# Sums of weight blocks formed by accumulating transfers, and five products of each FFN cut in two

## The chip, the cores and the metric

The kernel runs on one core of a Trainium2 chip. The metric is the device time of one execution in microseconds. A comparison uses the median of several runs.

## The reference

A decoder trunk of two layers over 256 positions of width 1024, in float32. Each layer has an FFN, a token-mixing sub-layer (a state-space branch and a delta-rule branch side by side), and a second FFN. The change touches only the four FFNs:

```python
def swiglu(x, w_in, w_out):
    gate, up = jnp.split(x @ w_in, 2, axis=-1)
    return (jax.nn.silu(gate) * up) @ w_out

for l in range(DEPTH):
    h = h + 0.5 * swiglu(rms_norm(h, ffn1_norm[l]), ffn1_w_in[l], ffn1_w_out[l])
    u = rms_norm(h, mix_norm[l])
    ...
    h = h + merged @ w_out[l]
    h = h + 0.5 * swiglu(rms_norm(h, ffn2_norm[l]), ffn2_w_in[l], ffn2_w_out[l])
return rms_norm(h, final_norm)
```

The inner width is 2816, that is 22 rows of 128 channels in `w_out`.

## The kernel before

**Numbers in two parts.** TensorE multiplies values of the type fp32r, which hold fewer bits than float32. So each float32 value is split into a high part, which ScalarE (ACT) makes by a copy, and a low part, which VectorE (DVE) makes by a subtraction. A product is three matmuls: high by high, high by low, low by high (`mm3`, `mm3w`). Weights are split on the chip: a raw tile of 128 x 1024 (512 KB) is loaded into `wraw` (five buffers, NRAW), `prep` makes `whi` and `wlo` (five buffers each, NSPL), and a product takes the pair with `take`.

**The plan.** `stream` lists the raw tiles in the order of their loads, and `plan` lists the forms in the order in which the products use them. `take` returns form j; before that it records the loads that are to be ahead of it and the `prep` of the forms up to j + 4. Each engine has a queue of its own that runs in order. The scheduler fills a queue by priority, which is program order, but when the next instruction has no free buffer it passes to a later one that has.

**An FFN** is the list `FFN`: one unit `f` with tokens as stationary side, then 20 units `c` (`chan_chunk`, two for each of ten channel pairs, 48 matmuls of 256 columns each), four block stages `A`, and the tail `BdBBBddddd`. `A` stands behind the 8th, 12th, 16th and 18th unit. Of the 22 rows of `w_out`, 16 are handled as eight pairs `PAIRS` by a scheme with seven instead of eight products of 2 x 2 blocks: rows are split in two channel blocks, columns in two halves of 512, tokens in two halves of 128. The activation's sums (`block_sums`) are made by DVE and ACT when a channel pair is done. The weights' sums are made from raw tiles that hold one block of two pairs: with b11, b12, b22 and b21 for the blocks, the products use b11, b12 - b11, b22 - b12 and b22 - b12 + b11 in `A` (forms `q0` to `q3`), and b22, b21 and b21 - b22 + b12 - b11 in `B` (`q4` to `q6`). A running sum lives in the tile `wfirst`, one of four slots `y0` to `y3` that are also used by the mixer. The subtractions are `less` in `prep`, on DVE: one each beside `q0`, `q1`, `q2` and `q4`, so 16 in an FFN. Those of `q1`, `q2` and `q4` stand between the ACT copy and the DVE split of that form.

Matmuls of a unit: for each half `a` of the channels, eight steps `kt` of three matmuls (L301 to L303) into one accumulator `fc`. Those of a block are L296 to L298 into `p` (stage `A`) or `o` (the tail). `join` adds the block accumulators into `h`; `close_blocks` runs the tail and ends with a group of five direct chunks. All other rows, `d`, are direct (`out_chunks`). All loads are issued by SyncE's queue (SP, L147). GpSimd (POOL) has little to do: the power in each norm (L190), a few others of the mixer.

Of the kernel before, what the change touches and what calls it, by code (L numbers as in the profile page):

```python
# [7 lines left out]
F32 = mybir.dt.float32  # L8
# [44 lines left out]
def trunk_kernel(ctx, tc, x, wst, wsm, norms, lpar, rpar, cst, out):  # L53
# [15 lines left out]
    def tt(o, a, b, op):  # L69
        return V.tensor_tensor(out=o, in0=a, in1=b, op=op)  # L70
# [29 lines left out]
    def plan_plain(j, n):  # L100
        for i in range(j, j + n):
            stream.append(i)
            plan.append(("d", [len(stream) - 1], len(stream)))
        return j + n

    def plan_ffn(j):


        o, j2, held = j + 4 * FC, j + 4 * FC + 22, []
        for kind in FFN:  # L110
            if kind in "fc":
                j = plan_plain(j, 4 if kind == "f" else 2)
            elif kind == "d":
                o = plan_plain(o, 1)
            else:
                if kind == "A":
                    where = [len(stream) + i for i in range(3)]
                    stream.extend(range(o, o + 3))
                    held.append((where, o + 2))
                    o += 4  # L120
                    for i, need in enumerate((2, 3, 3, 3)):
                        plan.append((f"q{i}", where, where[0] + need))
                else:
                    where, b22 = held.pop(0)
                    where += [len(stream) + 1, len(stream)]
                    stream.extend([b22, b22 + 1])
                    for i in range(4, 7):
                        plan.append((f"q{i}", where, len(stream)))
        return j2
# [6 lines left out]
    first = {js[0] for kind, js, _ in plan if kind == "q0"}  # L136
# [3 lines left out]

    def load(j):
        if j in first:
            r = slots.tile([P, 1024], F32, tag=f"y{state['first']}", name="wfirst")
# [3 lines left out]
        state["last"] = nc.sync.dma_start(r[:], wst[stream[j] // 2, :, (stream[j] % 2) * 1024 :][:, 0:1024])  # L147
        raws[j] = r

    def prep(i):  # L150
        kind, js, _ = plan[i]
        hi = wpool.tile([P, 1024], F32R, tag="whi", name="whi", bufs=NSPL)
        lo = wpool.tile([P, 1024], F32R, tag="wlo", name="wlo", bufs=NSPL)

        def less(o, a, b):
            tt(raws[js[o]][:], raws[js[a]][:], raws[js[b]][:], ALU.subtract)


        r = raws[js[{"q2": 1, "q4": 4, "q5": 3}.get(kind, 0)]]
        with ExitStack() as behind:  # L160
            for ins in state["behind"].pop(i, ()):
                behind.enter_context(tc.issue_after(ins))
            act(hi[:], r[:])
            if kind == "q1":
                less(1, 2, 1)
            elif kind == "q2":
                less(0, 2, 0)
            elif kind == "q4":
                less(0, 3, 0)
            tt(lo[:], r[:], f(hi[:]), ALU.subtract)  # L170
            if kind == "q0":
                less(0, 1, 0)
        for o in {"d": (0,), "q2": (1,), "q3": (2,), "q4": (4,), "q5": (3,), "q6": (0,)}.get(kind, ()):
            raws.pop(js[o])
        halves[i] = (hi, lo)

    def ahead(key, n, fn):
        while state[key] < n:
            fn(state[key])
            state[key] += 1  # L180

    def take():
        j = state["taken"]
        state["taken"] = j + 1
        ahead("loaded", min(plan[min(j + NSPL, n_forms) - 1][2] + NRAW - 1, n_raw), load)
        ahead("prepped", min(j + 1 if state["hold"] else j + NSPL, n_forms), prep)
        return halves.pop(j)
# [112 lines left out]
    def mm3w(ps, wh, wl, mh, ml, start, stop):  # L300
        PE.matmul(ps, wh, mh, start=start, stop=False)  # L301
        PE.matmul(ps, wh, ml, start=False, stop=False)  # L302
        PE.matmul(ps, wl, mh, start=False, stop=stop)  # L303
# [18 lines left out]
    def chan_chunk(ps):  # L322

        ws = [take(), take()]
        for a in range(2):
            for q in range(2):
                wh, wl = ws[q]
                for k in range(4):
# [9 lines left out]
                        kt == KT - 1,  # L338
                    )
# [48 lines left out]
    def join(pb):  # L388
# [6 lines left out]
        stt(u4[:], pb[5][:], 0.5, u2[:], ALU.mult, ALU.add)  # L395
        tt(hv[0][1], hv[0][1], u4[:], ALU.add)
        yield
        stt(u2[:], pb[7][:], 0.5, u2[:], ALU.mult, ALU.add)
        stt(u5[:], pb[5][:], 0.5, u2[:], ALU.mult, ALU.add)
        tt(hv[1][0], hv[1][0], u2[:], ALU.add)  # L400
        tt(hv[1][1], hv[1][1], u5[:], ALU.add)
# [27 lines left out]
    def ffn(nxt):  # L429
# [19 lines left out]
        def block_sums(p, g2):  # L449
# [34 lines left out]
        todo, pb, n = FFN[1:], {}, 0  # L484
        for c in range(FC - 1):
            g2 = tmp2("g2")
            for a in range(2):
                ps = accb("fc")
                chan_chunk(ps)
# [13 lines left out]
            if todo[0] == "A":  # L503
                if not pb:
                    pb.update({i: trb(f"p{i}") for i in (1, 6, 5, 7)})
# [7 lines left out]
                todo = todo[1:]  # L513
# [845 lines left out]
```

## Time and profile before

| | before |
|---|---|
| median of 3 runs | 1576.33 us (1573.42 to 1577.17) |
| the profiled execution's own time | 1574.73 us |
| span of that execution | 1573.0 us |
| TensorE busy | 1544.0 us, 98% |
| VectorE busy | 1254.2 us, 80% |
| ScalarE busy | 950.7 us, 60% |
| GpSimd busy | 53.8 us, 3% |
| read from HBM | 289.33 MB, 185 GB/s over the span |

How to read the lines: a group line gives the source line, the engine, the operation, the tile it writes and those it reads, the shape, the count, then the busy time in us, the mean of one in ns, and the engine's idle time ahead of it with what ended that. In a line of a stretch, each engine has its busy us and its count of instructions that touch the stretch; then come the clock that TensorE was granted (1.00 is full), the mean busy share of the 16 DMA engines, and GB/s. In a line in order of time, the first number is the start in us from the start of the span and the second is the duration; a bracket at the end gives the idle time before it and what released it. PE is TensorE and PEld its weight loads.

### The profile page before, as it was taken

The numbers are of one execution on the slowest core, as the hardware profiler recorded it, in microseconds if no ns is written. First come the engines' busy times: TensorE is split into PE (matmuls) and PEld (weight loads), VectorE is DVE, ScalarE is ACT, GpSimd is POOL, SyncE is SP. The second block draws the span as 40 slices with busy tenths as digits, with TensorE's granted clock in tenths as the row PEclk, the third lists the DMA queues.
The fourth block names the chain that finished last, engine by engine and source line by source line (L and its number), as shares of the span: only waits on it lengthen the run. The fifth ranks groups of instructions, "written<-read, shape, count | busy, mean of one in ns | idle before, by whom it ended". The sixth has DMA issues, their size and how long they took to land.

```text
span 1573.0 us, 28904 instructions
## 1 busy us (share of the span) xinstructions
PE 1544.0 (98%) x11432; PEld 1393.4 (89%) x11432; DVE 1254.2 (80%) x1888; ACT 950.7 (60%) x1534; POOL 53.8 (3%) x60
## 2 busy tenths in 40 slices
PE   8999999999999999999999999999999999999997
PEld 7999779999888888999789997899998888899995
DVE  6878868967899766878777888699589987677887
ACT  5656568766666645555555566776756665455554
POOL 0000010000000000000000001010000000000000
PEclk9999999999999999999999999999999999999999
DMA  8565565553565566565765456555345556555554
GB/s 297 199 201 186 185 213 188 168 164 114 180 212 164 183 205 192 169 207 181 243 206 191 166 186 223 192 188 188 115 137 200 175 185 215 176 191 187 161 186 133
DMA packets 94221, 293.12 MB, mean 186 GB/s; under 512 B 22325, under 2 KB 23301, under 8 KB 93062
## 3 DMA queue, kind: packets, MB, share of 16 engines
q1 hardware_dynamic: 94086, 291.29, 56.5%
q8 instruction: 89, 1.46, 0.4%
q14 instruction: 46, 0.38, 0.1%
HBM read 289.33 MB, written 1.92 MB: 185 GB/s over the span
## 4 chain that ended last, share of the span: by engine, by line
PE 68%; DVE 14%; DMA 7%; issue 5%; ACT 4%; POOL 1%; SPq 0%; POOLq 0%; ACTq 0%; DVEq 0%
PE fc L301 9%; PE fc L302 9%; PE fc L303 9%; DVE wlo L70 7%; DMA wraw<-in_wst_dram 4%; PE b L298 3%; PE t L297 3%; PE t L296 2%; PE t L298 2%; PE b L297 2%; PE b L296 2%; DVE ca L73 2%; ACT whi L67 2%; PE p L297 2%; PE p L298 2%
## 5 line engine op out<-in xcount | busy, mean ns | idle before, releaser
L70 DVE TENSOR_TENSOR wlo<-wraw,whi 128x1024 fp32r<-128x1024 f32 x488 | 592.3, 1222 | 176.8 <-ACT whi L67 172.3
L67 ACT ACTIVATE whi<-wraw 128x1024 fp32r<-128x1024 f32 x488 | 511.9, 1060 | 276.9 <-PE fc L302 96.0
L301 PE MATMUL fc<-uW,whi 128*128 128x256 f32 x1280 | 359.2, 281 | 0.0
L303 PE MATMUL fc<-uW,wlo 128*128 128x256 f32 x1280 | 358.9, 280 | 0.0
L302 PE MATMUL fc<-uW,whi 128*128 128x256 f32 x1280 | 358.9, 280 | 0.0
L303 PEld LDWEIGHTS fc<-uW,wlo 128*128 128x128 f32 x1280 | 243.6, 190 | 0.0
L301 PEld LDWEIGHTS fc<-uW,whi 128*128 128x128 f32 x1280 | 241.7, 189 | 0.8
L302 PEld LDWEIGHTS fc<-uW,whi 128*128 128x128 f32 x1280 | 240.3, 188 | 0.8
L67 ACT ACTIVATE whi<-wfirst 128x1024 fp32r<-128x1024 f32 x64 | 68.0, 1062 | 65.9 <-PE fc L302 50.9
L296 PE MATMUL t<-whi,uW 128*128 128x512 f32 x256 | 102.1, 400 | 0.0
L297 PE MATMUL t<-wlo,uW 128*128 128x512 f32 x256 | 100.6, 393 | 0.4 <-DVE wlo L70 0.4
L298 PE MATMUL t<-whi,uW 128*128 128x512 f32 x256 | 100.7, 393 | 0.0
L70 DVE TENSOR_TENSOR wlo<-wfirst,whi 128x1024 fp32r<-128x1024 f32 x64 | 78.3, 1223 | 8.8 <-ACT whi L67 8.8
L296 PE MATMUL b<-whi,bh 128*128 128x512 f32 x192 | 76.3, 399 | 0.3 <-ACT bh L67 0.2
L297 PE MATMUL b<-wlo,bh 128*128 128x512 f32 x192 | 74.9, 390 | 0.0
L298 PE MATMUL b<-whi,bl 128*128 128x512 f32 x192 | 74.3, 394 | 0.6 <-DVE bl L70 0.6
L70 DVE TENSOR_TENSOR wfirst<-wraw,wfirst 128x1024 f32<-128x1024 f32 x48 | 58.7, 1222 | 19.1 <-DMA wraw<-in_wst_dram 18.7
L301 PE MATMUL xs<-uW,whi 128*128 128x256 f32 x256 | 72.7, 284 | 0.0
L297 PE MATMUL o<-wlo,gh 128*128 128x512 f32 x160 | 64.5, 403 | 7.1 <-DVE wlo L70 6.9
L303 PE MATMUL xs<-uW,wlo 128*128 128x256 f32 x256 | 71.1, 278 | 0.0
L302 PE MATMUL xs<-uW,whi 128*128 128x256 f32 x256 | 71.0, 277 | 0.0
L296 PE MATMUL o<-whi,gh 128*128 128x512 f32 x160 | 62.1, 392 | 0.3 <-ACT whi L67 0.3
(315 smaller groups left out, 3385.8 us busy)
## 6 DMA issues: line engine op xcount, KB each, us to landing
wraw<-in_wst_dram SPq DMA_DIRECT2D x504, 512.0 KB, 4.5
wfirst<-in_wst_dram SPq DMA_DIRECT2D x16, 512.0 KB, 6.1
dc<-rdram SPq DMA_DIRECT2D x8, 1024.0 KB, 8.5
nw<-in_norms_dram SPq DMA_DIRECT2D x6, 512.0 KB, 5.9
gb<-rdram SPq DMA_DIRECT2D x8, 256.0 KB, 5.5
h<-in_x_dram SPq DMA_DIRECT2D x4, 256.0 KB, 5.9
out_dram<-fo SPq DMA_DIRECT2D x4, 256.0 KB, 2.0
dq<-X SPq DMA_DIRECT2D x2, 256.0 KB, 5.4
```

The source lines that it names most:

```text
L67: return A.activation(out=o, in_=i, func=func, **kw)
L70: return V.tensor_tensor(out=o, in0=a, in1=b, op=op)
L73: return V.scalar_tensor_tensor(out=o, in0=a, scalar=s, in1=b, op0=op0, op1=op1)
L296: PE.matmul(ps, lh, rh, start=start, stop=False)
L297: PE.matmul(ps, lh, rl, start=False, stop=False)
L298: return PE.matmul(ps, ll, rh, start=False, stop=stop)
L301: PE.matmul(ps, wh, mh, start=start, stop=False)
L302: PE.matmul(ps, wh, ml, start=False, stop=False)
L303: PE.matmul(ps, wl, mh, start=False, stop=stop)
```

## The change

It does three things, all in the FFNs.

- The weight sums are no longer made by DVE but by transfers that GpSimd issues, which add a block from HBM to a tile in SBUF. The signs are chosen so that all sums are plain sums: b11 + b12, then + b22, then + b21 in the tile of its own (now `wsum`), and b12 + b22 in a raw tile. Per group there are five plain loads as before (b11 twice, b12, b22 and b21) and four accumulating ones. The first two transfers of a group (`y` and its `+`) stand two characters of `FFN` ahead of `A` in the list of loads; the last two are issued after `q1` and `q3` are split.
- The products of `A` come in the order b11 + b12 (`q1`), b11 (`q0`), b12 + b22 (`q2`), b11 + b12 + b22 (`q3`). The signs of the activation's sums and of the joins follow.
- In five units of each FFN (the first of channel pair 1, and the one behind each `A`), the second matmul of the second step in the first half is issued as two of 128 columns.

```diff
+            if at in spots:
+                y = len(stream)
+                stream.extend([("y", o1 + 4 * q), ("+", o1 + 4 * q + 1, y)])
+                begun.append(y)
+                q += 1
...
+            elif kind == "A":
+                y, u = begun.pop(0), len(stream)
+                stream.extend([("w", o + 1), ("+", o + 2, u), ("w", o)])
+                plan.append(("q1", (y, o + 2), u))
+                plan.append(("q0", (u + 2,), u + 3))
+                plan.append(("q2", (u,), u + 3))
+                plan.append(("q3", (y, o + 3), u + 3))
+                held.append((y, o + 2))
+                o += 4
             else:
...
+                y, b22 = held.pop(0)
+                stream.append(("w", b22))
+                plan.append(("q4", (len(stream) - 1,), len(stream)))
+                stream.append(("w", b22 + 1))
+                plan.append(("q5", (len(stream) - 1,), len(stream)))
+                plan.append(("q6", (y,), len(stream)))
...
+    def add_to(r, i):
+        G.dma_start(out=r[:], in_=tile_of(i), accum_op=ALU.add)
...
     def prep(i):
...
             act(hi[:], r[:])
-            if kind == "q1":
-                less(1, 2, 1)
-            elif kind == "q2":
-                less(0, 2, 0)
-            elif kind == "q4":
-                less(0, 3, 0)
             tt(lo[:], r[:], f(hi[:]), ALU.subtract)
-            if kind == "q0":
-                less(0, 1, 0)
...
+        if kind in ("q1", "q3"):
+            add_to(r, js[1])
+        else:
+            raws.pop(js[0])
...
-    def mm3w(ps, wh, wl, mh, ml, start, stop):
+    def mm3w(ps, wh, wl, mh, ml, start, stop, cut=False):
         PE.matmul(ps, wh, mh, start=start, stop=False)
-        PE.matmul(ps, wh, ml, start=False, stop=False)
+        if cut:
+            PE.matmul(ps[:, :P], wh, ml[:, :P], start=False, stop=False)
+            PE.matmul(ps[:, P:], wh, ml[:, P:], start=False, stop=False)
+        else:
+            PE.matmul(ps, wh, ml, start=False, stop=False)
         PE.matmul(ps, wl, mh, start=False, stop=stop)
...
+                        cut and a == 0 and kt == 1,
...
-                chan_chunk(ps)
+                chan_chunk(ps, cut or (c, a) == (1, 0))
+                cut = False
...
-            tt(s1, a21, a22, ALU.add)
+            tt(s1, a21, a22, ALU.subtract)
-            tt(s4, a12, s2_, ALU.subtract)
+            tt(s4, a12, s2_, ALU.add)
...
                 four = [
+                    (pb[5], lambda p: sums(p, 0), PAIRS[n]),
                     (pb[1], lambda p: stat(2 * p, 0), PAIRS[n]),
-                    (pb[5], lambda p: sums(p, 0), PAIRS[n]),
                     (pb[7], lambda p: sums(p, 2), PAIRS[n]),
                     (pb[6], lambda p: sums(p, 1), PAIRS[n]),
                 ]
                 block_products(four, n == 0, n == len(PAIRS) - 1)
-                todo = todo[1:]
+                todo, cut = todo[1:], True
```

More of the change, by code (lines that the diff above doesn't have):

```diff
@@ L135, in trunk_kernel @@
     n_raw = len(stream)
-    first = {js[0] for kind, js, _ in plan if kind == "q0"}
+    limit = []
+    for _, _, need in plan:
+        m, room = need, NRAW
+        while m < n_raw:
+            room -= stream[m][0] == "w"
+            if not room:
+                break
+            m += 1
+        limit.append(m)
     n_forms = len(plan)
@@ L184, in take @@
         state["taken"] = j + 1
-        ahead("loaded", min(plan[min(j + NSPL, n_forms) - 1][2] + NRAW - 1, n_raw), load)
+        ahead("loaded", limit[min(j + NSPL, n_forms) - 1], load)
         ahead("prepped", min(j + 1 if state["hold"] else j + NSPL, n_forms), prep)
```

56 lines of the change are left out of this document (25 added, 31 removed).

## The prediction, made before the changed kernel was run

> **What bounds the kernel now.** I read the page first: the engines, then the chain.
>
> ```profile
> span 1573.0 us, 28904 instructions
> PE 1544.0 (98%) x11432; PEld 1393.4 (89%) x11432; DVE 1254.2 (80%) x1888; ACT 950.7 (60%) x1534; POOL 53.8 (3%) x60
> PE 68%; DVE 14%; DMA 7%; issue 5%; ACT 4%; POOL 1%; SPq 0%; POOLq 0%; ACTq 0%; DVEq 0%
> L301 PE MATMUL fc<-uW,whi 128*128 128x256 f32 x1280 | 359.2, 281 | 0.0
> L70 DVE TENSOR_TENSOR wfirst<-wraw,wfirst 128x1024 f32<-128x1024 f32 x48 | 58.7, 1222 | 19.1 <-DMA wraw<-in_wst_dram 18.7
> L70 DVE TENSOR_TENSOR wraw<-wraw 128x1024 f32<-128x1024 f32 x16 | 19.5, 1221 | 0.1
> ```
>
> TensorE is busy for 1544.0 of 1573.0 us, so freeing another engine can win back no more than 29 us, and only where TensorE idles. The subtractions that form the weight sums are 58.7 + 19.5 = 78.2 us of VectorE; that is the obvious target of the change and most of it is hidden. So the second question is how fast TensorE itself runs. A busy share cannot say that, but a count of matmuls in equal stretches can. I asked for the busy time by stretches of the channel units `fc`, which are alike everywhere:
>
> ```profile
> core 0: us, PE busy (x) PEld busy (x) DVE busy (x) ACT busy (x) POOL busy (x), PEclk, DMA share, GB/s
> 32.00:69.00 37.00, 37.00 (x317) 37.00 (x316) 27.82 (x45) 18.84 (x29) 0.00 (x0) 1.00 0.62 216
> 77.00:98.00 21.00, 21.00 (x181) 21.00 (x180) 16.48 (x25) 10.18 (x16) 0.00 (x0) 1.00 0.55 179
> 811.00:848.00 37.00, 37.00 (x329) 37.00 (x328) 28.88 (x46) 19.97 (x30) 0.00 (x0) 1.00 0.53 166
> ...
> core 0: us, PE busy (x), PEclk, DMA share, GB/s
> 625.00:662.00 37.00, 37.00 (x317) 1.00 0.52 163
> 1401.00:1438.00 37.00, 37.00 (x317) 1.00 0.51 162
> 1519.00:1528.00 9.00, 9.00 (x79) 1.00 0.62 198
> ```
>
> The rows at 32, 625, 811 and 1401 are the same units of the first, second, third and fourth FFN. TensorE is 100% busy at a granted clock of 1.00 in all, yet 37 us hold 317 matmuls in three FFNs and 329 in the third. A stretch counts every matmul that touches it, and one lasts 0.28 us (the 281 ns above), so the step is 37.28 / 317 = 0.1176 us against 37.28 / 329 = 0.1133 us. There is a long step and a short one, 4.3 ns apart, with no engine idle and nothing waited for. After a block stage the units have the long step: 21.28 / 181 = 0.1176 in the first such stretch, 9.28 / 79 = 0.1175 in the last, and the sixteen of them that I counted gave 181 in 21 us, 87 in 10 us or 79 in 9 us. What sets the cadence is seen in the order of time:
>
> ```profile
> 30.59 0.60 PE L498 MATMUL gT<-cs,sg 128*128 128x128 f32 x4
> 30.95 0.36 PE L301 MATMUL fc<-uW,whi 128*128 128x256 f32 x1
> 31.15 0.28 PE L302 MATMUL fc<-uW,whi 128*128 128x256 f32 x1
> 31.27 0.28 PE L303 MATMUL fc<-uW,wlo 128*128 128x256 f32 x1
> ...
> 809.74 0.60 PE L498 MATMUL gT<-cs,sg 128*128 128x128 f32 x4
> 810.09 0.37 PE L301 MATMUL fc<-uW,whi 128*128 128x256 f32 x1
> 810.87 0.28 PE L301 MATMUL fc<-uW,whi 128*128 128x256 f32 x1
> ...
> L498 PE MATMUL gT<-cs,sg x16: 272/272/273, 30.6 to 1399.7; 128*128 128x128 f32 x16
> ```
>
> The same four 128-column transposes stand ahead of the units with the long step at 30.95 and ahead of those with the short one at 810.09. So a few narrow products can leave the pipeline of weight loads and matmuls in either cadence, and it stays there until the next disturbance. It is stable, and it can be changed.
>
> **The change, part by part. 1, the cut products.** In each FFN five units have one 256-column product issued as two of 128 columns with the weights loaded twice: the first unit of channel pair 1 and the unit behind each of the four block stages, at the fifth matmul of the unit. That is 20 extra matmuls. The trace has no such product in fp32r. The nearest row is the transposes: four take 0.60 us and one alone 0.272 (the last line above), so the step is (0.60 - 0.27) / 3 = 0.11 us for 128 columns, hardly less than for 256, which says that the load of 128 weight columns sets it. Two cost 0.22, 0.10 more than the one: 20 x 0.10 = 2.0 us. Bounds: half of 0.1176 each, no cost; or 0.1176 each and one more step like the 0.20 us at 30.95, 0.20 x 20 = 4.0 us.
>
> What it may bring is the short step. While the two halves run, loads are the slower side and the matmuls wait for them; I read the short step as that condition (0.113 is nearly the 0.11 of the transposes) and the long one as loads that run ahead and matmuls that pay their own start. A cut would turn the one into the other. Ten matmuls go by before it holds (four ahead of the cut and some six to settle, as between 810.09 and 810.87). With 48 matmuls a unit, the stretches behind the cuts are six units, then 4, 4, 2 and 2: 278 + 182 + 182 + 86 + 86 = 814 matmuls an FFN. In the third the first stretch has the short step already, so 536 there, 3 x 814 + 536 = 2978 in all, x 4.3 ns = 12.8 us. All of it is on the path, for TensorE idles nowhere in these stretches. Bounds: nothing if the cadence does not turn, and 1.2 us lost (278 x 4.3 ns) if the cut also turns that stretch to the long step.
>
> The Trainium skill speaks against this part: TensorE: Matmul & The Clock Gate, section Back-to-back issue gap, gives a warm gap of N / 2.4 + 2.5 ns, which is 109 ns for 256 columns and 56 for 128. By it there is one cadence, a cut costs an estimated 2 ns, and 12.8 and 2.0 both drop out of the sum; the trace, with 117.6 and 113.3 at one width and one clock, does not agree.
>
> **2, VectorE's subtractions.** All 64 go, 16 an FFN. In the units and block stages nothing is gained (TensorE is gapless there). In the tails, where blocks and direct chunks finish an FFN, TensorE does wait:
>
> ```profile
> 160.00:193.00 33.00, 31.75 (x137) 24.55 (x136) 28.05 (x33) 19.14 (x23) 0.55 (x1) 1.00 0.60 201
> 753.00:787.00 34.00, 31.57 (x133) 24.11 (x133) 27.29 (x31) 18.67 (x22) 0.55 (x1) 1.00 0.75 257
> 938.00:970.00 32.00, 30.83 (x134) 24.30 (x132) 27.44 (x32) 19.13 (x22) 0.55 (x1) 1.00 0.59 201
> 1529.00:1566.00 37.00, 34.52 (x146) 26.30 (x144) 29.93 (x35) 18.48 (x23) 0.55 (x1) 1.00 0.42 139
> ...
> 764.33 1.23 DVE L70 TENSOR_TENSOR wfirst<-wraw,wfirst 128x1024 f32<-128x1024 f32 x1 [1.93 <-DMA wraw<-in_wst_dram]
> ...
> 766.75 0.50 PE L297 MATMUL o<-wlo,gh 128*128 128x512 f32 x1 [0.95 <-DVE wlo L70]
> ```
>
> The idle time is 1.25 + 2.43 + 1.17 + 2.48 = 7.3 us, the most that can come back. At 764.33 the subtraction for the form `q4` waits 1.93 us for the second block and takes 1.23, with the split of `q4` queued behind it, and TensorE then waits 0.95 us. After the change the split follows at once. The later waits of a tail come from five splits in a row and from the join, which stay. I take one subtraction of 1.22 us in half of the time for each tail: 4 x 0.6 = 2.4 us gained.
>
> **3, the accumulating transfers.** Each of the 16 groups keeps its five loads of 512 KB on SP's queue and gets four accumulating ones on GpSimd's; the first of its sums, b11 + b12, is begun ahead of the group in a slot of its own. The trace has no accumulating transfer and none issued by GpSimd.
>
> ```profile
> q1 hardware_dynamic: 94086, 291.29, 56.5%
> DMA to landing us min/median/max: 3.3/4.5/9.3
> dc<-rdram SPq DMA_DIRECT2D x8, 1024.0 KB, 8.5
> ...
> 60.53 1.23 DVE L70 TENSOR_TENSOR wlo<-wfirst,whi 128x1024 fp32r<-128x1024 f32 x1 [0.25 <-ACT whi L67]
> 69.27 1.06 ACT L67 ACTIVATE whi<-wfirst 128x1024 fp32r<-128x1024 f32 x1 [2.05 <-PE fc L302]
> 70.37 1.23 DVE L70 TENSOR_TENSOR wlo<-wfirst,whi 128x1024 fp32r<-128x1024 f32 x1 [0.19 <-ACT whi L67]
> 74.95 0.39 PE L297 MATMUL p<-wlo,bsa 128*128 128x512 f32 x1
> ```
>
> The second line is that of the weight loads. An accumulation reads what it adds and the tile, and writes the tile: I take its time from issue to landing as the 8.5 us of 1024 KB, between 3.3 (the fastest plain load) and 18.6 (twice the slowest). Share of the queue: 64 x 0.524 MB = 33.6 MB more, 33.6 / 291.29 x 56.5% = 6.5% of the span, 13% if each costs double; there is room. The tight one is the addition of b22 between the splits of `q1` and `q3`. In the first block stage the first form's split ends at 60.53 + 1.23 = 61.76; the fourth form is wanted at 74.95, and 1.23 + (70.37 - 69.27) before that, at 72.62, its ACT copy must start. So 10.9 us are free, more than 8.5: cost nothing. Were that cover gone, the copy would stand at the head of ACT's queue, with the next units' splits and activations behind it, and TensorE would wait for it. For b12 + b22 and the early sum the loads are issued further ahead.
>
> The Trainium skill, DMA: Bandwidth & Descriptors, section Anatomy of one DMA — SWDGE (gpsimd) path, fits 2.0 us + bytes / 436e3 for transfers issued by GpSimd, an estimated 3.2 us for 512 KB without the addition; no run here shows one, and it would also leave this part at nothing.
>
> One place is worse. The early sums start as soon as their slots are free, and between the second and the third FFN, which adjoin, this is in the tail:
>
> ```profile
> 752.37 0.33 SPq L147 DMA_DIRECT2D wfirst<-in_wst_dram  x1
> ...
> 771.87 0.33 SPq L147 DMA_DIRECT2D wfirst<-in_wst_dram  x1
> 785.44 0.55 POOL L190 TENSOR_TENSOR zz<-zz,mhalf 128x1 f32<-128x1 f32 x1 [176.32 <-DVE zz L78]
> ```
>
> Those are the first and the last of the four loads. That tail already has a DMA share of 0.75 at 257 GB/s, 8.7 MB in 34 us. Four additions bring 2.1 MB, 0.18 of share at plain price and 0.36 at double, and then it is over 1 by 0.11, 3.8 us. Between 0 and 3.8 I take 1.5 us, since the last falls behind the tail. GpSimd has queued behind these additions the power of the norm at 785.44; a load issued at 771.87 has landed by 781.2 at the slowest, so it isn't late.
>
> The moved signs swap additions for subtractions, the same count; the new order of the forms asks for block sums made several units before. No cost.
>
> **Sum**, against the profiled execution's own 1574.73 us (span 1573.0): 1574.73 - 12.8 + 2.0 - 2.4 + 1.5 = 1563.0 us. The three runs lie between 1573.42 and 1577.17 with the median 1.6 us above the profiled one, less than I can size, so I forecast 1563 for the median.
>
> **The rivals.** First, the cuts do not turn the cadence. For it: behind 128-column products both steps occur (30.95, 810.09). Against: the cut adds no change of shape that lets loads run ahead. Then 1574.73 + 2.0 - 2.4 + 1.5 = 1575.8, no change; with the dear ends (4.0 for the cuts, 3.8 in the tail, nothing gained from the subtractions) up to 1582.5. The skill's rule above would give this outcome too.
>
> Second, the cadence turns in some places only, say half: 1563.0 + 6.4 = 1569.4.
>
> Third, slower: the addition of b22 lands late, in 16 places. It decides from 10.9 us on. At 13 us each block stage stops TensorE for 2.1, 34 us in all, so 1563 + 34 = 1597; at 18.6 it is 123 us. The break-even is 10.9 + 12 / 16 = 11.7 us. For it: one plain load took 9.3, and additions share the engines with loads at shares of 0.5 to 0.75. Against: 1 MB took 8.5.
>
> **How the numbers follow.** The forecast 0.60, cadence in some places 0.10, no turn 0.13, late additions 0.17. The range goes from 1555 (cuts free and all 7.3 us of tail idle won: 1574.73 - 12.8 - 7.3 = 1554.6) to 1580, which takes in the first two rivals nearly whole and leaves out the late additions and the dearest no-turn ends, under 0.2. About 0.3%, 4.7 us, is what a measurement here can tell from no change. Faster is the forecast and the half turn, 0.70; same the no turn but for its dear ends, 0.10; slower the rest, 0.20.
>
> **What would show it.** Right: 37 us of the first units hold 329 matmuls in all four FFNs and 21 us behind a block stage some 187 instead of 181; the two sum groups of VectorE are gone; no copy `whi` waits for an addition; TensorE's idle time is unchanged outside the tails. Wrong: 317 and 181 as before, or rows in which ACT waits for a DMA ahead of the fourth block form and `p` has idle time before it.

## The result: slower by 0.3%, and the profile after

| | before | after |
|---|---|---|
| median | 1575.49 us (1573.42 to 1579.58, 10 runs) | 1580.08 us (1578.05 to 1581.63, 10 runs) |
| ratio | | 1.0028, interval 1.0018 to 1.0039 |
| the profiled execution's own time | 1574.73 us | 1578.05 us |

I had forecast 1563.0. The change costs 4.6 us, where 12 were to be won. First the page of after: engines, DMA queues, and the DMA issues (count, KB each, median us from issue to landing).

```profile
span 1576.3 us, 29059 instructions
PE 1538.9 (98%) x11452; PEld 1391.0 (88%) x11452; DVE 1187.5 (75%) x1824; ACT 946.0 (60%) x1534; POOL 110.5 (7%) x124
q1 hardware_dynamic: 94086, 291.29, 55.4%
q0 software_dynamic: 9216, 33.56, 12.1%
wsum<-in_wst_dram POOLq DMA_DIRECT2D x48, 512.0 KB, 8.3
wraw<-in_wst_dram POOLq DMA_DIRECT2D x16, 512.0 KB, 8.1
```

VectorE lost 66.7 us of work and TensorE 5.1, and the span is 3.3 us longer. So TensorE waits more than before. The 64 accumulating transfers take 8.3 and 8.1 us from issue to landing (medians), close to the 8.5 I had taken, and q0's share is inside the forecast's 6.5 to 13%.

Then the units, by stretches, as before the change:

```profile
31.00:68.00 37.00, 37.00 (x329) 37.00 (x328) 24.66 (x42) 19.13 (x30) 5.39 (x6) 1.00 1.02 303
75.50:96.50 21.00, 21.00 (x186) 20.96 (x185) 15.17 (x24) 11.37 (x17) 1.75 (x2) 1.00 0.96 280
620.00:657.00 37.00, 37.00 (x329) 37.00 (x328) 25.78 (x42) 19.94 (x29) 1.76 (x2) 1.00 0.74 216
```

The counts are 329 where they were 317, and 186 where they were 181, so the short step is there. Behind the block stages it comes with the cut, as forecast. In the first units it isn't the cut's doing: in all four FFNs of after the step, from start to start, is 113.3 ns in the unit ahead of the cut already (the experiment on the cadence comes back to this).

New are waits in the block stages. TensorE's idle time before the matmuls into `p` was nothing in before; in after it is (us, times, by what ended it):

```profile
  ACT whi L67: 7.3, 4
  DVE wlo L70: 3.8, 5
```

In the order of time, the fourth block stage of the first FFN shows the chain, here VectorE, GpSimd, ScalarE and TensorE one after the other:

```profile
130.15 1.22 DVE L70 TENSOR_TENSOR wlo<-wraw,whi 128x1024 fp32r<-128x1024 f32 x1
...
135.44 1.22 DVE L70 TENSOR_TENSOR wlo<-wsum,whi 128x1024 fp32r<-128x1024 f32 x1
137.18 0.87 POOL L165 DMA_DIRECT2D wsum<-in_wst_dram  x1 [5.53 <-ACT whi L67]
146.65 1.06 ACT L67 ACTIVATE whi<-wsum 128x1024 fp32r<-128x1024 f32 x1 [7.05 <-DMA wsum<-in_wst_dram]
141.12 0.39 PE L315 MATMUL p<-whi,bsb 128*128 128x512 f32 x1
...
144.99 0.39 PE L317 MATMUL p<-whi,bsb 128*128 128x512 f32 x1
147.76 0.50 PE L315 MATMUL p<-whi,bsb 128*128 128x512 f32 x1 [2.38 <-ACT whi L67]
149.02 0.51 PE L316 MATMUL p<-wlo,bsb 128*128 128x512 f32 x1 [0.76 <-DVE wlo L70]
```

Read it from the top. The fourth stage begins at 141.12, only two units (11.0 us) behind the third, which so ends at 130.1. The third has freed the split buffers of its forms one right behind the other, and VectorE works them off together with the sums of the activation: ten instructions without a gap from 130.15 on, of which the first and the last are shown. The split of the fourth stage's `q1` is the last and ends at 136.66. Only then may GpSimd issue the addition of b22 to the same tile. (The bracket of its row names a copy of ScalarE. That of `q1` had ended at 133.75, though, and in all four FFNs this issue comes 0.5 us after the end of the split.) It needs 9.5 us (137.18 to 146.65). TensorE would have wanted the next product at about 145.2, so the copy 1.1 us earlier (147.76 less 146.65), at 144.1. From 137.18 that is 6.9 us of cover, or 7.4 from the end of the split, from which the prediction had counted its 10.9. The addition is 2.6 us late, and that is the 2.38 in the row. Counted in the same way from the end of the split, the fourth stages of FFN 2, 3 and 4 have 9.2, 8.2 and 9.2 us of cover, and their copies start 10.3, 10.0 and 11.8 us after it.

It has a second price. Right behind, the granted clock is down; here are the five stretches of 7 us around all such places (the clock is the third number from the right):

```profile
150.00:157.00 7.00, 7.00 (x48) 6.86 (x48) 5.57 (x7) 3.82 (x5) 0.13 (x1) 0.76 0.90 219
740.00:747.00 7.00, 6.92 (x40) 6.49 (x41) 6.63 (x8) 4.40 (x5) 0.86 (x1) 0.76 0.72 162
791.00:798.00 7.00, 7.00 (x28) 5.65 (x27) 6.28 (x10) 5.18 (x9) 0.00 (x0) 0.76 0.82 211
931.00:938.00 7.00, 7.00 (x46) 6.86 (x45) 5.92 (x7) 4.09 (x6) 0.47 (x1) 0.76 0.83 205
1522.00:1529.00 7.00, 6.69 (x40) 6.20 (x41) 6.87 (x8) 4.65 (x6) 0.86 (x1) 0.76 0.69 146
```

A mean of 0.76 over 7 us is 3.4 us at half clock and the rest at full, so 1.7 us are lost in each, 8.5 in all. Before had none but in its last 3 us. Four begin in or right behind the fourth block stage of the four FFNs, one is in the norm between FFN 2 and FFN 3. The Trainium skill, TensorE: Matmul & The Clock Gate, section Part 1: The HAM clock gate, says that the clock falls to half after an idle window of about 3.4 us and comes back after a busy one of that length. The size agrees. The trigger was shorter here: waits of 2.38 and 0.76 us with one matmul between them were enough, and in FFN 2 of 0.86 and 0.76. But in the kernel with the sums alone (below) 1.25 and 0.76 us in the same stage of FFN 1 were not followed by half clock, so what exactly sets it off is not shown.

The fifth place has a cause of its own:

```profile
766.83 13.21 SPq L177 DMA_DIRECT2D wraw<-in_wst_dram  x7
780.13 0.38 SPq L177 DMA_DIRECT2D wsum<-in_wst_dram  x1
788.24 0.86 POOL L165 DMA_DIRECT2D wsum<-in_wst_dram  x1 [14.16 <-DMA wsum<-in_wst_dram]
788.80 0.88 POOL L209 TENSOR_TENSOR zz<-zz,mhalf 128x1 f32<-128x1 f32 x1
```

The last of the four early loads of FFN 3 is issued at 780.13, not at 771.87 as before; its addition waits for it at the head of GpSimd's queue until 788.24; and the norm's power, which all of TensorE's work of FFN 3 waits for, stands right behind it. TensorE idles for 2.56 us there. The load's own slot had been free since 769.09, when the split of what it held ended. The load stood in SyncE's queue behind the seven loads of raw tiles in the first row.

To say where the time went, I added up the profiled executions from the first matmul of each part to the first of the next, and up to the last matmul of the kernel:

| us | units `f`, `fc` | block stages | tails and the mixers' ends | rest of the mixers |
|---|---|---|---|---|
| before | 506.0 | 87.2 | 195.3 | 767.5 |
| after less before | -8.4 | +15.7 | -5.2 | +1.2 |

### The profile page after: what moved, and what is told of

Its sections match the earlier page's. It is cut to its first block, busy times and chain, and to the rows that moved or that the text cites. A ratio compares the mean times of both kernels' runs of the same rounds, so it can differ in the third digit from the quotient of the medians.

```text
span 1576.3 us, 29059 instructions
## 1 busy us (share of the span) xinstructions
PE 1538.9 (98%) x11452; PEld 1391.0 (88%) x11452; DVE 1187.5 (75%) x1824; ACT 946.0 (60%) x1534; POOL 110.5 (7%) x124
## 3 DMA queue, kind: packets, MB, share of 16 engines
q0 software_dynamic: 9216, 33.56, 12.1%
## 5 line engine op out<-in xcount | busy, mean ns | idle before, releaser
L70 DVE TENSOR_TENSOR wlo<-wraw,whi 128x1024 fp32r<-128x1024 f32 x504 | 611.3, 1220 | 209.3 <-ACT whi L67 201.4
L67 ACT ACTIVATE whi<-wraw 128x1024 fp32r<-128x1024 f32 x504 | 526.7, 1058 | 277.8 <-PE fc L325 83.7
L320 PE MATMUL fc<-uW,whi 128*128 128x256 f32 x1280 | 356.1, 278 | 0.0
L325 PE MATMUL fc<-uW,whi 128*128 128x256 f32 x1260 | 349.6, 277 | 0.0
L70 DVE TENSOR_TENSOR wlo<-wsum,whi 128x1024 fp32r<-128x1024 f32 x48 | 58.7, 1222 | 54.7 <-ACT whi L67 53.6
L67 ACT ACTIVATE whi<-wsum 128x1024 fp32r<-128x1024 f32 x48 | 50.8, 1058 | 66.8 <-DMA wsum<-in_wst_dram 46.7
L165 POOL DMA_DIRECT2D wsum<-in_wst_dram x48 | 43.3, 901 | 344.6 <-DVE wlo L70 200.4
```

The costliest lines, as they stand in the source:

```text
L67: return A.activation(out=o, in_=i, func=func, **kw)
L165: G.dma_start(out=r[:], in_=tile_of(i), accum_op=ALU.add)
```

## The experiments

Eleven kernels, each beside the kernel before. Where there are several runs, the ratio to it has a 95% interval; three kernels have one run.

**The two halves of the change, one by one.** The cuts alone, put into the kernel before:

```diff
-        PE.matmul(ps, wh, ml, start=False, stop=False)
+        if cut:
+            PE.matmul(ps[:, :P], wh, ml[:, :P], start=False, stop=False)
+            PE.matmul(ps[:, P:], wh, ml[:, P:], start=False, stop=False)
+        else:
+            PE.matmul(ps, wh, ml, start=False, stop=False)
```

> Only the cut products, with the sums on VectorE as before. Theory 1 (the cuts earn what was forecast, and the loss is made in two places by the accumulating transfers): the channel units gain 3.3 us in the first, second and fourth FFN and 2.1 in the third, 12 us in all; 1575.5 - 12 = 1563.5 us, a ratio of 0.992, granted clock as before (0.999), 187 matmuls in 21 us behind each block stage. Rival (the denser matmuls are what makes the clock drop, not the waits): stretches at half clock appear here too, mean clock about 0.994, and of the 12 us some 8 are given back: 1571 us.

Measured 1565.81 us (1564.88 to 1569.24) against 1574.14, ratio 0.9945 (0.9931 to 0.996). The units take 11.4 us less, all block stages stay at 5.45, no stretch at half clock. FFN 2's tail grew by 1.5 us and FFN 3's by 1.1. About 7.8 of the 11.4 us lie behind the block stages, where all sixteen stretches have the short step. The other 3.7 lie in the first units, and there the short step stands ahead of the cut in FFN 1, 2 and 4. Only in FFN 3 does it come with the cut; here are stretches of 5 us ahead of it and behind it:

```profile
805.00:810.00 5.00, 5.00 (x45) 1.00 0.71 235
812.00:817.00 5.00, 5.00 (x47) 1.00 0.61 208
```

So behind the block stages the cuts do what they were forecast to do, and denser matmuls by themselves do not bring the clock down.

The sums alone are the kernel after without its cuts:

```diff
-                chan_chunk(ps, cut or (c, a) == (1, 0))
+                chan_chunk(ps)
```

> Only the accumulating transfers with their signs and order, no product cut. Theory 1: what is lost is here, about 16 us: 3 to 5 us in the fourth block stage of each FFN (ACT waits for the addition of b22) with half a window of clock behind it, 4 us and a delayed norm between the second and the third FFN, less 2 to 4 us in each of the other three tails: 1580.1 + 12 = 1592 us, a ratio of 1.010. Rival (only the two edits together lose, because the quicker units leave the transfers too little time): the waits ahead of the fourth block stage are nearly gone and the time is at or below that of the kernel before, 1570 to 1576 us.

Measured 1577.91 us (1575.51 to 1583.53), ratio 1.0026 (1.0013 to 1.0039). The 1592 was far off: by themselves the sums lose 3.8 us, not 18. That is with some luck: in the profiled execution the first units of FFN 1, 2 and 4 have the short step with no cut at all, which makes the first units 2.9 us shorter than in before. The block stages cost 6.2 us more than in before, and one stretch at half clock stands in FFN 2's tail. The idle time before `p` is

```profile
  DVE wlo L70: 3.0, 4
  ACT whi L67: 1.3, 1
```

The two halves do not add up: -8.3 and +3.8 make -4.5, and both together gave +4.6. The fourth stages are 1.0 to 2.6 us longer than in before with the sums alone, and 2.9 to 4.8 with both, and only then does the clock fall behind each of them. The first units are a part of this: their gain stands in both halves, 3.7 and 2.9 us, and only once in the whole, 3.9 (profiled executions). In the fourth stages it is the cover that shrank. Counted from the end of the split it is 8.9, 10.5, 10.5 and 10.5 us with the sums alone and 7.4, 9.2, 8.2 and 9.2 with both. The additions there land 9.7 to 9.9 us after their issue with the sums alone and 9.3 to 9.6 with both, so they did not slow down but in FFN 4 (11.2).

**Is it the addition or GpSimd's queue?** The same kernel with plain transfers from GpSimd. It leaves the additions out: the second block overwrites the first.

```diff
-        G.dma_start(out=r[:], in_=tile_of(i), accum_op=ALU.add)
+        G.dma_start(out=r[:], in_=tile_of(i))
```

> The kernel after, with the accumulating transfers turned into plain ones from the same queue: the second block overwrites the first and no sum is formed, so that the output is another; everything else, the order of issues and the waits included, is the same. Theory (the addition itself, which reads and writes the block in place, is what makes the transfer long): landing of the 64 transfers goes from a median of about 8.2 us to 5 to 6, the fourth stages from 8.3 to 10.2 us to under 6.5, the time to 1564 to 1570. Rival (GpSimd's queue is what is slow, its writing of descriptors and its turn behind the sixteen other queues): landing stays at 7.5 to 8.5 us, the fourth stages stay over 8, and the time is within 4 us of the kernel after.

```profile
span 1552.4 us, 29059 instructions
q0 software_dynamic: 9216, 33.56, 6.9%
wsum<-in_wst_dram POOLq DMA_DIRECT2D x48, 512.0 KB, 5.0
wraw<-in_wst_dram POOLq DMA_DIRECT2D x16, 512.0 KB, 6.0
wraw<-in_wst_dram SPq DMA_DIRECT2D x504, 512.0 KB, 5.0
```

Measured 1554.21 us, one run, 10 below what I expected. All sixteen stages take 5.45 us, no clock is lost, the units take 11.4 us less and the tails 10.0 less. A plain transfer from GpSimd lands in 5.0 to 6.0 us, about as fast as one from SP. So the addition is what costs: 2.1 to 3.3 us more from issue to landing, and 1.75 times the DMA share (12.1 to 6.9%). The rival, a slow queue, falls. The norm behind FFN 2 is late here too, by 1.70 us of idle TensorE: the last early load is issued at 768.08, though its slot was free at 759.10, and its GpSimd transfer again stands ahead of the power. The Trainium skill, Collectives: The Full Stack, section The bandwidth ceiling: the fold count and why AG ≠ RS ≠ AR, says of a reducing collective within a chip that it is slower for its two source reads and not for the add itself. The factor here is near its two; that the cause is the same is not shown by these runs.

**Is it the place of the stages?** First the gaps moved: two narrow ones ahead of the second and third stage, four units ahead of the fourth.

```diff
-FFN = "f" + 8 * "c" + "A" + 4 * "c" + "A" + 4 * "c" + "A" + 2 * "c" + "A" + 2 * "c" + "BdBBBddddd"
+FFN = "f" + 8 * "c" + "A" + 2 * "c" + "A" + 2 * "c" + "A" + 4 * "c" + "A" + 4 * "c" + "BdBBBddddd"
```

> The kernel after, with the four block stages that sum weight blocks set behind 8, 10, 12 and 16 units instead of 8, 12, 16 and 18: the two narrow gaps are now the first two, the last two stages have four units between them. Nothing is left out. Theory (an addition is issued when q1's split of the stage before frees VectorE's and ScalarE's reading of the previous block, and needs some 8 to 9 us; two units and the rest of a stage leave about 8 us): the second and third stage of each FFN now take 8 to 10 us instead of 5.4, the fourth goes from 8.3 to 10.2 back to 5.4; the time stays within 6 us of the kernel after or comes out longer by up to 10, since two narrow gaps stand in each FFN. Rival (the fourth stage is late because of what follows it, the first product of the second kind of block stage, and not because of the two units ahead of it): the fourth stage stays at 8 us or more, the second and third at 5.4.

Measured 1606.15 us, one run. The second stage takes 7.9 us in FFN 1 and 5.9 to 6.1 in the others, the third 12.0 to 13.4 in all four (some matmuls of the next unit stand between its products and are not counted), the fourth 5.7 to 6.5. TensorE's long wait there is again for ScalarE's copy of a late sum:

```profile
111.75 0.50 PE L315 MATMUL p<-whi,bsa 128*128 128x512 f32 x1 [4.30 <-ACT whi L67]
113.01 0.79 PE L316 MATMUL p<-wlo,bsa 128*128 128x512 f32 x1 [0.76 <-DVE wlo L70]
```

So the delay moved to the narrow gaps, as the theory says, but it is worst in the second of them, and the time is longer by 26 us than that of after, not by up to 10. The rival, that what follows the fourth stage makes it late, falls.

Then no narrow gap at all:

```diff
+FFN = "f" + 6 * "c" + "A" + 4 * "c" + "A" + 4 * "c" + "A" + 4 * "c" + "A" + 2 * "c" + "BdBBBddddd"
```

> The changed kernel with the block stages behind the 6th, 10th, 14th and 18th channel unit, so that four units lie between any two (before: behind the 8th, 12th, 16th and 18th). Bytes and instructions are the same. Theory 1 (the addition of b22 has too little time only where two units lie between two stages): no TensorE idle time in any block stage, no half clock behind them, 14.5 + 5 us won: 1580.1 - 19.5 = 1560.5 us, ratio 0.990; the norm between the second and the third FFN is still delayed. Rival (the sum of the traffic is what costs, wherever it lies): the block stages still wait, in other places, and the time stays within 4 us of 1580.

Measured 1568.65 us (1566.76 to 1574.48), ratio 0.9966 (0.9955 to 0.9977). Fifteen of sixteen stages take 5.45 us: the waits at the fourth stage are gone in all FFNs. Two places were left. FFN 2's tail took 39.6 us, with the norm behind an addition as in after. And FFN 1's first stage took 13.4 us:

```profile
30.00:40.00 10.00, 10.00 (x90) 10.00 (x89) 7.44 (x13) 5.45 (x9) 1.02 (x1) 1.00 1.02 325
50.00:60.00 10.00, 10.00 (x80) 9.60 (x79) 2.92 (x6) 2.31 (x5) 1.78 (x2) 1.00 1.05 270
60.00:70.00 10.00, 4.51 (x13) 2.48 (x12) 4.43 (x6) 4.15 (x6) 0.88 (x1) 0.77 0.55 143
```

The last two numbers of a line are DMA share and GB/s. At the start all four slots are free, all early loads and additions go at once, the DMA engines are full (1.02 to 1.05), and the loads for the first stage, now two units earlier, come late.

To hold those early loads back I made each one wait for the load ahead of it in the stream:

```diff
-        state["last"] = nc.sync.dma_start(r[:], tile_of(i))
+        with ExitStack() as behind:
+            if kind == "y":
+                behind.enter_context(tc.issue_after(state["last"].ins))
+            state["last"] = nc.sync.dma_start(r[:], tile_of(i))
```

> As the run with the spread stages, and the early load of b11 keeps its place in SyncE's queue behind the load ahead of it in the list, so that it is not issued in the tail of the FFN before. Theory 1 (between the second and the third FFN the norm's power waits in GpSimd's queue behind an addition, which waits for that load): GpSimd's queue is free at that norm, the tail of the second FFN falls from 41.5 us to the 33.6 of the others and the half clock there is gone: 9 to 10 us below the run with the spread stages, 1551 us, ratio 0.984. Rival (the tail is late because its own weight loads are, behind the additions' bytes): the tail falls by 2 us at most.

Measured 1578.81 us (1575.66 to 1581.17), ratio 1.0026 (1.0016 to 1.0036). FFN 2's tail fell to 33.9 us and has no half clock any more. This doesn't single out the norm, since no early load or addition at all is left in that tail. In the trace of the spread order the norm's wait is 1.94 us, and the tail's own late products wait 0.78 and 0.76 us and are followed by half clock, another 1.7. So both theory and rival have a part in the 5.7 us. But the stages took 24.2 us more than in before: now every early sum is formed just ahead of its stage, and two additions stand one behind the other in GpSimd's queue. A middle way, each early load behind the place of the group before:

```diff
+                stream.extend([("y", o1 + 4 * q, anchor), ("+", o1 + 4 * q + 1, y)])
+                anchor = y - 1
...
+                behind.enter_context(tc.issue_after(issued[stream[j][2]].ins))
```

> The spread order of the run before last (6, 10, 14 and 18 units ahead of the four stages), with each group's first load put behind the load at which the group before stands in the stream, so that it is issued one group ahead and not as soon as a buffer is free, and not right behind its neighbour either. Nothing is left out. Theory (two separate losses: an addition that starts too late for its stage, and a first load and additions that come all at once at the start of an FFN or stand in GpSimd's queue ahead of the norm's power): all block stages at 5.4 to 6 us, the tail between FFN 2 and FFN 3 at 34 instead of 39.6, FFN 1's first stage under 8 instead of 13.4, time 1552 to 1558. Rival (GpSimd's queue runs its transfers one after the other, so that any order which gives each addition its turn late in a group makes ScalarE wait): stages of 7 to 9 us again as in the held order, time 1565 to 1580.

Measured 1574.23 us (1567.84 to 1576.99), ratio 0.9995 (0.9978 to 1.0012): my 1552 to 1558 missed. FFN 2's tail was 34.1 as expected, but the third and fourth stages took 5.5 to 8.7 us, and the second of FFN 1 7.2. The rival's numbers came. Whether GpSimd's queue or the DMA engines make the additions late there was not separated; either way an early sum that isn't urgent costs least when it is formed long before.

**A better version?** Hold only the loads that do harm:

```diff
+HELD = [{2: 10, 3: 24}, {}, {3: 7}, {}]
...
+            if kind == "y" and stream[j][2] is not None:
+                behind.enter_context(tc.issue_after(issued[stream[j][2]].ins))
```

> The spread order (6, 10, 14 and 18 units ahead of the four stages), with only three of the sixteen first loads held back: in FFN 1 that of the third group behind the eleventh load of the FFN and that of the fourth behind the load with index 24, so that the transfers at the start are not all at once, and in FFN 3 that of the fourth group behind the load with index 7, so that its addition can't stand in GpSimd's queue ahead of the norm's power. All others go as early as a slot is free, so that additions that aren't urgent are done before those that are. Nothing is left out. Theory (what the spread order still lost are these two places alone: 8.0 us and two stretches at half clock in FFN 1's first stage, 5.7 us in FFN 2's tail): FFN 1's first stage under 8 us, all others at 5.4 to 6, FFN 2's tail at 34, and 1568.65 less 8 to 12 and less 5.7, so 1551 to 1556. Rival (whatever holds a first load puts its addition ahead of an urgent one, as in the two held orders): FFN 1's stages 7 to 9 us each again, 1560 to 1568.

Measured 1566.46 us (1564.08 to 1572.8), ratio 0.9955 (0.994 to 0.997). The time is within the rival's range. FFN 1's first stage took 9.6 us and its fourth 7.1, the fourth of FFN 3 6.6, and FFN 2's tail 37.7, now no longer for the norm:

```profile
770.00:775.00 5.00, 3.77 (x17) 2.76 (x15) 1.94 (x3) 1.97 (x2) 0.00 (x0) 1.00 1.04 272
775.00:780.00 5.00, 4.24 (x12) 3.15 (x12) 1.63 (x2) 0.72 (x2) 0.00 (x0) 0.67 1.03 372
780.00:785.00 5.00, 5.00 (x24) 4.12 (x22) 1.67 (x4) 2.18 (x4) 0.56 (x1) 0.99 0.27 109
```

The tail's own loads meet the other early sums of FFN 3 at a DMA share of 1.03, and right behind it stands the norm with 0.27. So the last version moves all four early loads of FFN 3 there, and gives FFN 1 its stages behind 8, 12, 16 and 20 units:

```diff
+FIRST = "f" + 8 * "c" + "A" + 4 * "c" + "A" + 4 * "c" + "A" + 4 * "c" + "A" + "BdBBBddddd"
+HELD = [{}, {}, {0: 6, 1: 8, 2: 10, 3: 24}, {}]
```

> As the staggered run, with two places changed again. FFN 1 has its four stages behind 8, 12, 16 and 20 units and none of its first loads held (it has one cut less, since no unit follows its last stage). In FFN 3 all four first loads are held, behind its loads with index 6, 8, 10 and 24, so that they fall behind the tail of FFN 2, where the staggered run showed a DMA share of 1.0, and into the norm, where it showed 0.27. Nothing is left out. Theory (the loss left is that of transfers crowded where the DMA engines are full): FFN 1's stages 5.4, 5.4, 6.6 and 5.5 us, FFN 2's tail 34 instead of 37.7, no stretch at half clock, 1566.5 less 4.2, 1.7 and 3.4 for FFN 1 and 3.7 for the tail, so 1552 to 1556. Rival (held loads make their additions collide with urgent ones): FFN 3's stages 7 to 9 us, 1558 to 1566.

Measured 1561.78 us (1557.84 to 1566.14), ratio 0.9921 (0.9904 to 0.9938): faster than before and after, and the best of all that were made with the whole computation. FFN 2's tail took 33.6 us and FFN 1's first three stages 5.6 to 5.8; no stretch at half clock was left. It is 6 to 10 us short of what I expected and within the rival's range: the third and fourth stages of FFN 3 took 6.8 and 6.0 us, the fourth of FFN 4 7.5, and FFN 1's last stage with its tail 41.4, two more than the parts make elsewhere.

Whether the spread order needs the sums at all, the cuts alone in that order tell:

> The kernel before with the cuts and with the four stages behind 6, 10, 14 and 18 units, its sums still made by VectorE. Nothing is left out. It tells what of the gain of the spread orders belongs to the place of the stages and not to the sums. Theory (the stages are late only because of the additions, and VectorE's sums cost only in the tails): all stages at 5.4, tails as in the kernel before, 1562 to 1569, the same as the cuts alone (1565.81). Rival (the spread order itself eases the tails or the first stage): under 1560.

Measured 1567.7 us (1566.07 to 1570.5), ratio 0.996 (0.9946 to 0.9974). All stages at 5.45, the tails as in before or longer (37.4, 40.2, 36.4 and 37.0 us). So the place alone gains nothing, and what the best version has over the cuts comes from the tails of FFN 2 to 4, which are 1.8 to 4.4 us shorter than in before (33.6, 33.9 and 33.6 against 37.9, 35.7 and 36.9). By the medians it is 4 us faster than the cuts alone (1561.78 and 1565.81), but the intervals of the two ratios just overlap, so this gain is not shown beyond the noise.

**What turns the cadence?** The cut product, issued twice over all 256 columns (it counts twice):

```diff
-            PE.matmul(ps[:, :P], wh, ml[:, :P], start=False, stop=False)
-            PE.matmul(ps[:, P:], wh, ml[:, P:], start=False, stop=False)
+            PE.matmul(ps, wh, ml, start=False, stop=False)
+            PE.matmul(ps, wh, ml, start=False, stop=False)
```

> The kernel before, with each of the five places not cut in two halves of columns but issued twice over the full 256 columns (that product counts twice, so the output is another): 20 more matmuls of 256 columns, no narrow ones. Theory (a product of 128 columns ends sooner than the load of the next weights, so that the order of loads and products slips by one step and the step falls from 0.1176 to 0.1133 us): a full product doesn't turn it, the units keep 0.1176 behind the place, and the time is 2 us longer than the kernel before. Rival (any product without a weight load of its own turns the step): 0.1133 behind each place as with the cut, and 10 us less in the units.

The same two stretches, first with the cut (the cuts alone), then with the doubled product:

```profile
75.50:96.50 21.00, 21.00 (x188) 21.00 (x187) 16.78 (x25) 10.75 (x16) 0.00 (x0) 1.00 0.55 181
620.00:657.00 37.00, 37.00 (x329) 37.00 (x328) 28.56 (x46) 19.84 (x31) 0.00 (x0) 1.00 0.55 174
```

```profile
75.50:96.50 21.00, 21.00 (x181) 21.00 (x180) 16.39 (x25) 10.05 (x16) 0.00 (x0) 1.00 0.56 188
620.00:657.00 37.00, 37.00 (x329) 37.00 (x328) 27.31 (x42) 20.99 (x31) 0.00 (x0) 1.00 0.58 187
```

Measured 1572.57 us, one run. Behind all sixteen block stages the step stays long (181, as in before), so there a further matmul alone does not turn it, and two narrow ones do. In the first units of all four FFNs the step is short, but there it already was from the transposes on, ahead of the doubled product: that stretch falls into either cadence by itself, as it had in FFN 3 of before.

This bears on every kernel here. Without a single cut, the first units are 4.0 us shorter than in before, which fits with the time not being the 2 us longer that I expected. The 3.7 us that the kernel with the cuts alone won in the same units can't be put down to its cuts. Over the thirteen profiled kernels, the step of the first units is short ahead of any cut in 41 of 52 FFNs. In seven of the other eleven a cut follows, and it turns the step to the short one each time; the other four are in kernels without cuts. With one profiled execution of each kernel, it is not shown whether the step of these units belongs to a kernel or changes from run to run. Why two narrow products turn the order of loads and matmuls is not shown either; that they do is.

## Why the prediction was wrong, step by step

**1, the cut products: right behind the block stages, and luck in the first units.** Forecast were -12.8 and +2.0, so -10.8 us, and the cuts alone took 11.4 from the units. Behind the block stages the forecast comes to 7.6 (536 matmuls in each of four FFNs at 4.3 ns, less 16 cuts at 0.10 us), and 7.8 came, with 188 matmuls where some 187 were forecast. The cost of a cut was near enough: three products with a cut took 0.46 us (810.17 to 810.63 in the cuts alone), without one 0.34, so 0.12 where 0.10 was taken. For the first units the forecast comes to 3.2. There 3.7 came, but a kernel without narrow products has 4.0, so the number fits and the cause doesn't. The step took the long cadence of before for a property of these units, though its own rows had both behind the same transposes. What was not in the step: 2.6 us came back in two tails, which, as I read it, are fed by loads and reach their waits earlier. The first rival, no turn, falls behind the block stages. The Trainium skill's formula (TensorE: Matmul & The Clock Gate, section Back-to-back issue gap) was the wrong one to hold against this part: the section gives it for an isolated matmul and says that in a stream of weight loads and matmuls both set the spacing.

**2, VectorE's subtractions: right in sign, mis-sized.** I took 0.6 us from each tail, 2.4 in all and 7.3 at most. With plain transfers in the place of additions the tails gave 10.0, of which 1.8 was lost again between the last matmul and the end (8.9 us instead of 7.1). The 7.3, TensorE's idle time in the tails, was thus no upper bound.

**3, the accumulating transfers: this step failed, at the cover first and at the price in part.** I took their cost as nothing. The time of an addition, 8.5 us, was right as a median (8.3), but in the fourth stages they took 9.3 to 11.2, with 0.5 us ahead of the issue. I worked the cover out in the first block stage, 10.9 us, and used it for all sixteen. There it held (10.9 in after too, and 9.5 used). The fourth stage has only two units ahead of it, and its `q1` split stands in VectorE's backlog behind the third stage: 7.4 to 9.2 us of cover, where 10.0 to 11.8 were needed. The list `FFN` showed those two units, and the stage most pressed was the one to work out. The third rival named the mechanism but priced it as sixteen equal places from 10.9 us on; in truth it struck mainly four (14.5 of the 15.7 us), from 7.4 on. And no step had that waits of 1.6 to 3.2 us then cost 1.7 more by the clock: 8.5 us in the five places.

**The tail between FFN 2 and FFN 3.** Forecast +1.5 for the traffic, measured +3.6 in all. The step took the load to be issued at 771.87, as in before, and so the norm's power not to be late. But the load was issued at 780.13, 11.0 us after its slot was free, since it stood behind seven others in SyncE's queue, and the power stood behind its addition: 2.56 us, and 1.7 at half clock. With plain transfers the load is 9.0 us behind its slot, so the slow additions are not the main cause of that. That GpSimd's queue holds the norm was seen; that the changed kernel moves the very load was not.

**The sum.** Without the additions' cost the kernel takes 1554.21 (one run), under the 1563 of the sum, so it had missed on both sides: 9 us too little gained in the tails, and 26 us of additions at nothing. The Trainium skill's fit for transfers issued by GpSimd (DMA: Bandwidth & Descriptors, section Anatomy of one DMA — SWDGE (gpsimd) path) gave an estimated 3.2 us for a plain one; beside the other traffic 5.0 to 6.0 are measured here.

## What to carry to other kernels

A transfer that must start after one use of a tile and end before the next has a cover that differs from place to place: work it out where the neighbours stand closest, with the backlog of the engine that gives the start, not where it is easiest to read. Work moved from an engine with slack to the DMA engines isn't free when these are full at moments, and it is moved well only if it can be done long before it is needed. Test the halves of a change apart: here one half alone was 8 us faster, and the other hid it and took 4 more. And look at a stretch ahead of the change as well as behind it: some of those 8 us also come without the change.

## What the runs showed of the hardware that was not expected

- An accumulating transfer of 512 KB takes 8.1 to 8.3 us (medians) where a plain one from the same queue takes 5.0 to 6.0, and 1.75 times the share of the DMA engines.
- Two short waits of TensorE close together were followed by 3.41 us at a granted clock of 0.5, four times in after (from 0.86 and 0.76 us to 2.42 and 0.75), and a fifth time behind one wait of 2.56 us. Ahead of the end of the kernel there is no half clock in before, in the cuts alone or with plain transfers. In the staggered version 1.23 and 0.76 us, in a tail, did the same; 1.25 and 0.76 us in the sums alone did not.
- A run of 256-column products has two cadences, 117.6 and 113.3 ns, at full clock; one product issued as two of 128 columns leads from the long one into the short one at all sixteen places behind a block stage of the cuts alone, and a doubled full product at none. In other kernels some cuts did not turn it: two that were issued at half clock (one of them behind the fourth stage of FFN 2 in after), one at full clock in the held order, and most of those in the narrow order that stand among a stage's own products.
